# Modulation sums on TensorE in column groups, activations loaded first: a fused transformer block pair, 256 tokens, one core

## The chip, the cores and the metric

The kernel runs on one core of a Trainium2 chip. It is one launch that computes two transformer blocks in float32. The metric is the device time of a launch in microseconds (us); three runs of the kernel before took 879.94 us in the median.

## The reference

Cut to what matters. `c` is one vector of 1024, `x` has 256 tokens of 1024.

```python
c_act = jax.nn.silu(c)
mod = c_act @ w_ada[l] + b_ada[l]                    # w_ada: 1024 x 6144
sh1, sc1, g1, sh2, sc2, g2 = jnp.split(mod, 6, axis=-1)
h = modulate(rms_norm(x, norm1_w[l]), sh1, sc1)      # h * (1 + sc1) + sh1
mix = hybrid_mixer(h, w_in[l], ...)                  # h @ w_in first: q, k, v, z, gates, short conv
x = x + g1[:, None, :] * mix
h = modulate(rms_norm(x, norm2_w[l]), sh2, sc2)
x = x + g2[:, None, :] * swiglu(h, w_ffn_in[l], w_ffn_out[l])
shf, scf = jnp.split(c_act @ w_ada_f + b_ada_f, 2, axis=-1)
...
```

The mixer has a gated delta rule with 8 heads (keys, queries, values, a triangular inverse for each head and half of the tokens), a short convolution branch, and gates. A second block (attention and a gated feed-forward) follows. Nothing of the first block's products with `w_in` can start before `sh1` and `sc1`, which need two of the six column blocks of `w_ada`, 4 MB each.

## The kernel before, in words

All products keep the channels on the 128 partitions and the 256 tokens in the free dimension. A float32 product is made of three matmuls in the faster `fp32r` format: each weight tile is split into a high part `whi` (a copy by ScalarE) and a low part `wlo` (a subtraction by VectorE), and the activations likewise (`h1h`, `h1l` for the first block's input). A tile product is `whi*h1h + whi*h1l + wlo*h1h`. So each unit of work (128 columns of a weight matrix, 8 tiles deep, 24 matmuls) needs one `whi` copy and one `wlo` subtraction of 128x1024 ahead of it. Behind stage one the planner makes these at most five units ahead (`SPL`). Weights come in chunks of up to 1 MB into four buffers `raw` over SyncE's DMA queue, in the order of the list `chunks`; a buffer is loaded again when its last reader is done.

**Stage one** (the loop `for kt in range(KT)`, eight rounds) makes the first input and its first products at once. In round `kt` it takes the 128 columns of `sh1` and of `sc1` that belong to channels `128*kt ...` (chunk `2*kt`, 1 MB of `w_ada`, laid out as [2 vectors, 8 row blocks, 128 columns]) and the 128 rows of `w_in` that those channels multiply (chunk `2*kt+1`). The two sums over 1024 rows are shared by two engines: VectorE multiplies the first 5 or 6 row blocks by `cact` (silu of `c`, one column for each row block) and adds them into `acc` (`gemv_v`, table `gvs`), and TensorE does the remaining row blocks with the weights as the stationary tile and one column of `cact` as the moving one (`gemv`), then adds `acc` over the partitions with a column of ones (`gemv_sum`). `first_mod` adds the bias and makes the scale `a1`. VectorE and ScalarE then make `h1h` and `h1l` for this `kt`, and TensorE adds this channel block's share to six open PSUM banks (`su_mm`, 36 matmuls a round). In the order of the code, round `kt` issues `gemv(kt)`, most of `su_mm(kt-1)`, `gemv_sum(kt)`, the rest of `su_mm(kt-1)`.

**Behind stage one** a planner in Python writes the instruction order: it keeps an estimated clock for each engine (`account`), and between the matmuls of the units it emits what its clock says is ready. Each engine then runs its own list strictly in that order and waits where an operand or a buffer isn't ready. Units follow in the order of the list `units`: the remaining short-convolution columns, the gate columns SCB, two pairs of z, the short-convolution output, the value columns V (with z between), queries Q, gates, and so on. The **later modulation vectors** (`g1`, `sc2`, `sh2`, `g2`, and the two of the last norm) are summed by VectorE alone, four chunks of 1 MB for each vector, two row blocks a chunk: one operation of 128x1024 for each row block into `acc` (`ada_chunk`). `ada_finish` then turns `acc` with eight transposes on TensorE (`sd<-cn,acc`) into two PSUM banks and reduces it with two `TENSOR_REDUCE` into `mod`. Where a chunk stands is set by calls of `sprinkle()` in the list of units. Small PSUM banks for such side work (`sd`) are four and are taken in turn. For the keys, `pair_products` (`sd<-KQ`) and then VectorE's `junk`, `ssk`, `wsc` and `AK` operations run head by head; when all heads are done, `small_inverses` runs 62 small VectorE operations, and later `inverse` (tile `TX`) goes back and forth between TensorE, ScalarE and VectorE.

In the trace nearly every instruction has line L136, the recording helper; so rows are told apart by their tiles.

Of the kernel before, what the change touches and what calls it, by code (L numbers as in the profile page):

```python
# [11 lines left out]
F32 = mybir.dt.float32  # L12
F32R = mybir.dt.float32r
AF = mybir.ActivationFunctionType
OP = mybir.AluOpType
AX = mybir.AxisListType

P = 128
D = 1024
# [51 lines left out]
def body(ctx, tc, a, out):  # L71
# [190 lines left out]
    def bank():  # L262
        i = freeb.popleft()
        return i, pss.tile([P, 512], F32, name=f"sd{i}", tag=f"sd{i}", bufs=1)
# [28 lines left out]
    ones = cst.tile([P, 1], F32, name="ones")  # L293
    V.memset(ones, 1.0)

    colA = cst.tile([P, P], F32, name="colA")
    colB = cst.tile([P, P], F32, name="colB")
    colC = cst.tile([P, P], F32, name="colC")
    colD = cst.tile([P, P], F32, name="colD")
    cact = cst.tile([P, KT], F32, name="cact")  # L300
    mod = cst.tile([P, 8, KT], F32, name="mod")
    a1 = cst.tile([P, KT], F32, name="a1")
# [1260 lines left out]
    def sprinkle():  # L1563
        if later:
            ada_chunk(*later.popleft())
# [12 lines left out]
    for jp in range(4):  # L1578
        pair_units(w_in, SCB0, jp, post_b, h1)
        if jp % 2 == 0:  # L1580
            sprinkle()
    for jp in range(2):
# [3 lines left out]
    for jp in range(4):  # L1586
        pair_units(w_in, V0, jp, post_v, h1)
        if jp < 2:
            pair_units(w_in, Z0, 2 + jp, post_z, h1)
        else:  # L1590
            sprinkle()
    for jp in range(4):
# [51 lines left out]

    load_chunks(1)
    for t in range(2):
        SY.dma_start(xtok[:, t], a["x"][0, t * P:(t + 1) * P, :])
    load_chunks(RAW)
    i, b = bank()
    PE.transpose(b[:, :P], va, ident)  # L1650
# [3 lines left out]
    freeb.append(i)  # L1654
    A.activation(cact, colA[:, 104:112], AF.Silu)

# [3 lines left out]

    def gemv(kt, gv):
        rv = chunks[2 * kt]["v"].rearrange("p (v r) c -> p v r c", v=2)
        i, b = su_b[kt] = bank()
        for v in range(2):
            for r in range(gv, KT):
                PE.matmul(b[:, v:v + 1], rv[:, v, r, :], cact[:, r:r + 1], start=(v == 0 and r == gv), stop=False,
                          skip_group_check=True)

    def gemv_v(kt, r0, r1):
        rv = chunks[2 * kt]["v"].rearrange("p (v r) c -> p v r c", v=2)  # L1670
        ak = ac4[:, kt % 2]
        for r in range(r0, r1):
            if r == 0:
                V.tensor_scalar(ak, rv[:, :, 0, :], cact[:, 0:1], None, op0=OP.mult)
            else:
                V.scalar_tensor_tensor(ak, rv[:, :, r, :], cact[:, r:r + 1], ak, op0=OP.mult, op1=OP.add)

    def gemv_sum(kt):
        i, b = su_b.pop(kt)
        for v in range(2):  # L1680
            PE.matmul(b[:, v:v + 1], ac4[:, kt % 2, v], ones, start=False, stop=True, skip_group_check=True)
        return i, b

    def first_mod(kt, i, b):
        V.tensor_tensor(mod[:, 0:2, kt], b[:, 0:2], colA[:, kt:16:8], OP.add)
        freeb.append(i)
        V.scalar_tensor_tensor(a1[:, kt:kt + 1], mod[:, SC1, kt:kt + 1], 1.0, colA[:, 64 + kt:65 + kt],
                               op0=OP.add, op1=OP.mult)

    gemv(0, 5)  # L1690
    gemv_v(0, 0, 5)
    chunks[0]["free"] = et["V"]
    i, b = gemv_sum(0)
    first_mod(0, i, b)
    ss = wk.tile([P, 2], F32, name="rm", tag="rm")
    rs = wk.tile([P, 2], F32, name="rr", tag="rr")


    scr = slot.tile([P, KT * S + 16], F32, name="scr", tag="L")[:, :D]
    for t in range(2):  # L1700
        A.activation(scr, xtok[:, t], AF.Square, accum_out=ss[:, t:t + 1])
    V.tensor_scalar(ss, ss, 1.0 / D, EPS, op0=OP.mult, op1=OP.add)
# [10 lines left out]
    def x_copied(kp, i, b):  # L1713
        V.tensor_copy(xT[:, 2 * kp:2 * kp + 2].rearrange("p k t -> p (k t)"), b)
        freeb.append(i)

    for kp in range(2):
        x_copied(kp, *x_turned(kp))
    for j in range(3):
        rows(vb, 96 + j * 8, a["sc_conv_w"][0, j], G)  # L1720
# [35 lines left out]
    freeb.append(i)  # L1756
    x_rest = [(kp, *x_turned(kp)) for kp in (2, 3)]
    split_hi(0, (0,))

# [43 lines left out]

    gvs = [5] + [5] * 3 + [6] * 4 + [0]
    for kt in range(KT):
# [3 lines left out]
        if kt:  # L1809
            gemv(kt, gvs[kt])  # L1810
            chunks[2 * kt]["free"] = et["V"]
        load_chunks(2 * kt + 1 + RAW)
        if kt:
            split_hi(kt)
        if kt > 1:
            su_mm(kt - 1, range(NB - 2))
        n1 = n2 = 0
        if kt:
            i, b = gemv_sum(kt)
            low_of(kt, 0)  # L1820
            if 4 <= kt < KT - 1:
                n1, n2 = 0, 1
                gemv_v(kt + 1, 0, n1)
            first_mod(kt, i, b)
# [9 lines left out]
        if kt:  # L1834
            low_of(kt, 1)
        gemv_v(kt + 1, n1, n2)
        V.scalar_tensor_tensor(h1l[:, kt], t, shc, h1h[:, kt].bitcast(F32), op0=OP.add, op1=OP.subtract)
        if not kt:
            low_of(0, 0)
            low_of(0, 1)  # L1840
        if kt < KT - 1:
            gemv_v(kt + 1, n2, gvs[kt + 1])
        give(t)
# [143 lines left out]
```

## Time and profile before

| | before |
|---|---|
| median of 3 runs | 879.94 us (878.63 to 882.96) |
| profiled execution, its own time | 880.14 us |
| its span in the trace | 878.4 us |
| mean granted TensorE clock | 0.988 of full |
| TensorE matmul busy | 841.7 us (96%), 6847 records |
| VectorE busy | 694.2 us (79%) |
| ScalarE busy | 497.9 us (57%) |
| DMA, mean | 202 GB/s |

The time is 1.7 us over the span in the profiled execution. Busy shares are means over stages: TensorE's 96% says that it hardly waits anywhere, and the few places where it does are looked for in windows. A float32 matmul stands in the trace as two records, an `fp32r` matmul or a transpose as one.

### The profile page before, as it was taken

Reading aid. Unit: us, or ns where it says so; the run is one execution under the profiler, and the core shown is the slowest. Engines: PE = TensorE matmul, PEld = TensorE weight load, DVE = VectorE, ACT = ScalarE, POOL = GpSimd, SP = SyncE. Lnnn points to the kernel's source line nnn. Section 1 sums busy time; section 2 is a strip of 40 time slices with the busy share of each in tenths; the row PEclk is TensorE's granted clock in tenths of the full one; section 3 lists DMA queues with packets and bytes.
Section 4 is the critical chain, followed back from the end, with each engine's and each line's share of the span. In section 5 each row is a group of like instructions: output and inputs, shape, how many; then the busy total and the mean of one; then the engine's idle time right before and its main releaser. Section 6 shows DMA issues by size and latency. Waiting matters only on the chain.

```text
span 878.4 us, 17105 instructions
## 1 busy us (share of the span) xinstructions
PE 841.7 (96%) x6847; PEld 812.8 (93%) x6847; DVE 694.2 (79%) x1314; ACT 497.9 (57%) x902; POOL 70.9 (8%) x83
## 2 busy tenths in 40 slices
PE   6999988999999999999999999999999989999995
PEld 6999987999999999999999999998899989999884
DVE  5899998899758889889977555888748988988452
ACT  3349653456656645575554453668656747766341
POOL 3200231000001200200000010200004000000000
PEclk9999998999999999999999999999999989999998
DMA  9995765567724787759988586643425464554611
GB/s 289 317 298 180 247 229 169 168 218 215 240 63 148 230 287 234 261 173 302 326 285 286 169 276 213 207 144 106 136 96 193 132 217 156 192 192 168 199 65 48
DMA packets 158063, 177.35 MB, mean 202 GB/s; under 512 B 9052, under 2 KB 143584, under 8 KB 157984
## 3 DMA queue, kind: packets, MB, share of 16 engines
q1 hardware_dynamic: 156000, 172.57, 61.0%
q0 software_dynamic: 1472, 3.06, 1.1%
q8 instruction: 54, 0.88, 0.4%
q10 hardware_dynamic: 512, 0.62, 0.2%
q14 instruction: 25, 0.20, 0.1%
HBM read 174.64 MB, written 1.60 MB: 201 GB/s over the span
## 4 chain that ended last, share of the span: by engine, by line
PE 56%; issue 22%; DVE 16%; ACT 5%; DMA 1%; POOL 0%; SPq 0%; POOLq 0%; ACTq 0%; DVEq 0%
PE mm L136 48%; PE sd L136 8%; DVE wlo L136 5%; DVE acc L136 3%; DVE cv L136 2%; ACT whi L136 2%; DVE sct L136 1%; DMA raw<-in_w_ada_dram 1%; ACT L136 0%; DVE junk L136 0%; DVE gx L136 0%; DVE AK L136 0%; ACT KQ L136 0%; ACT ct L136 0%; ACT cv L136 0%
## 5 line engine op out<-in xcount | busy, mean ns | idle before, releaser
L136 DVE TENSOR_TENSOR wlo<-raw,whi 128x1024 fp32r<-128x1024 f32 (+2 forms) x267 | 319.3, 1203 | 84.0 <-ACT whi L136 83.6
L136 ACT ACTIVATE whi<-raw 128x1024 fp32r<-128x1024 f32 (+2 forms) x267 | 274.0, 1033 | 152.1 <-PE mm L136 129.0
L136 PE MATMUL mm<-h1h,whi 128*128 128x256 f32 x552 | 159.8, 292 | 0.4 <-ACT h1h L136 0.2
L136 PE MATMUL mm<-h1h,wlo 128*128 128x256 f32 x552 | 153.2, 280 | 1.8 <-DMA raw<-in_w_in_dram 1.3
L136 PE MATMUL mm<-h1l,whi 128*128 128x256 f32 x552 | 153.6, 280 | 0.5 <-DVE h1l L136 0.3
L136 PEld LDWEIGHTS mm<-h1h,whi 128*128 128x128 f32 x552 | 104.6, 191 | 1.7 <-ACT h1h L136 1.1
L136 PEld LDWEIGHTS mm<-h1h,wlo 128*128 128x128 f32 x552 | 103.8, 189 | 2.4 <-DVE wlo L136 2.2
L136 PEld LDWEIGHTS mm<-h1l,whi 128*128 128x128 f32 x552 | 104.0, 189 | 1.4 <-DVE h1l L136 1.1
L136 PE MATMUL mm<-ynh,whi 128*128 128x256 f32 x288 | 82.3, 286 | 4.2 <-DVE gx L136 4.2
L136 PE MATMUL mm<-ynl,whi 128*128 128x256 f32 x288 | 81.8, 284 | 0.0
L136 PE MATMUL mm<-h2nh,wlo 128*128 128x256 f32 x288 | 79.9, 277 | 1.9 <-DVE wlo L136 1.9
L136 PE MATMUL mm<-ynh,wlo 128*128 128x256 f32 x288 | 81.7, 284 | 0.0
L136 PE MATMUL mm<-h2nh,whi 128*128 128x256 f32 x288 | 80.2, 279 | 0.0
L136 PE MATMUL mm<-h2nl,whi 128*128 128x256 f32 x288 | 79.8, 277 | 0.0
L136 DVE SCALAR_TENSOR_TENSOR acc<-raw,cact,acc 128x1024 f32<-128x1024 f32 (+1 forms) x78 | 72.2, 925 | 1.5
L136 PEld LDWEIGHTS mm<-ynh,whi 128*128 128x128 f32 x288 | 55.9, 194 | 4.3 <-issue 4.3
L136 PE MATMUL mm<-xah,whi 128*128 128x258 f32 x192 | 57.2, 298 | 0.0
L136 PEld LDWEIGHTS mm<-h2nh,wlo 128*128 128x128 f32 x288 | 54.1, 188 | 2.1 <-DVE wlo L136 2.1
L136 PEld LDWEIGHTS mm<-ynh,wlo 128*128 128x128 f32 x288 | 55.6, 193 | 0.0
L136 PEld LDWEIGHTS mm<-ynl,whi 128*128 128x128 f32 x288 | 55.4, 192 | 0.0
L136 PE MATMUL mm<-xal,whi 128*128 128x256 f32 x192 | 54.4, 283 | 0.0
L136 PEld LDWEIGHTS mm<-h2nh,whi 128*128 128x128 f32 x288 | 54.3, 189 | 0.0
(335 smaller groups left out, 2107.0 us busy)
## 6 DMA issues: line engine op xcount, KB each, us to landing
raw<-in_w_in_dram SPq DMA_DIRECT2D x30, 1024.0 KB, 5.1
raw<-in_w_ffn_in_dram SPq DMA_DIRECT2D x22, 1024.0 KB, 7.5
raw<-in_w_up_dram SPq DMA_DIRECT2D x22, 1024.0 KB, 5.1
raw<-in_w_ada_dram SPq DMA_DIRECT2D x16, 1024.0 KB, 5.3
raw<-in_w_qkv_dram SPq DMA_DIRECT2D x12, 1024.0 KB, 5.2
raw<-in_w_down_dram SPq DMA_DIRECT2D x10, 1024.0 KB, 5.0
raw<-in_w_ada_dram SPq DMA_DIRECT2D x16, 512.0 KB, 6.5
raw<-in_w_o_dram SPq DMA_DIRECT2D x8, 1024.0 KB, 5.8
```

The costliest lines, as they stand in the source:

```text
L136: r = fn(*args, **kw)
```

## The change: order of loading, TensorE's column groups, and two chunks elsewhere

Three edits. First, the two loads of `x` go ahead of the first `w_ada` chunk on SyncE's queue, and the two squares for the norm are split around the silu, which now writes `cact32`, every value of `cact` 32 times. Second, `gemv` is turned round: 32 equal columns of `cact32` are the stationary tile and the weights move (128 or 256 columns), eight matmuls that write to partitions 0, 32, 64 and 96 in turn (four column groups of the array); ScalarE copies the bank to `acc`, and `gemv_sum` multiplies with `sel`, which has a one at partitions 0, 32, 64 and 96, so that the four groups are added. VectorE's share (`gemv_v`) is gone. In round 0 the eight matmuls are issued for each vector apart, behind the transposes of `x`. Third, the `sprinkle()` of the SCB loop is gone, and that of the V loop runs in all four turns in place of two: the third and fourth chunk of `g1` move there.

```diff
     for jp in range(4):
         pair_units(w_in, SCB0, jp, post_b, h1)
-        if jp % 2 == 0:
-            sprinkle()
...
         if jp < 2:
             pair_units(w_in, Z0, 2 + jp, post_z, h1)
-        else:
-            sprinkle()
+        sprinkle()
...
-    load_chunks(1)
     for t in range(2):
         SY.dma_start(xtok[:, t], a["x"][0, t * P:(t + 1) * P, :])
     load_chunks(RAW)
...
+    A.activation(scr, xtok[:, 0], AF.Square, accum_out=ss[:, 0:1])
...
-    A.activation(cact, colA[:, 104:112], AF.Silu)
+    A.activation(cact32, colA[:, 104:112, None].to_broadcast([P, KT, 32]), AF.Silu)
+    V.tensor_copy(cact, cact32[:, :, 0])
+    A.activation(scr, xtok[:, 1], AF.Square, accum_out=ss[:, 1:2])
...
+    def gemv(kt, vs):
         rv = chunks[2 * kt]["v"].rearrange("p (v r) c -> p v r c", v=2)
-        i, b = su_b[kt] = bank()
-        for v in range(2):
-            for r in range(gv, KT):
-                PE.matmul(b[:, v:v + 1], rv[:, v, r, :], cact[:, r:r + 1], start=(v == 0 and r == gv), stop=False,
-                          skip_group_check=True)
...
+        for r in range(KT):
+            g = 32 * (r % 4)
+            PE.matmul(b[g:g + 32, vs[0] * P:vs[0] * P + w].rearrange("p (v c) -> p v c", c=P), cact32[:, r],
+                      rv[:, vs[0]:vs[0] + len(vs), r], start=(r < 4 and vs[0] == 0), stop=(r >= 4 and vs[-1] == 1),
+                      skip_group_check=True)
+        et["PE"] -= (et["PE"] - t0) * 0.75
+        if vs[-1] == 1:
+            A.activation(ac4[:, kt % 2].rearrange("p v c -> p (v c)"), b[:, 0:2 * P], AF.Copy)
+            chunks[2 * kt]["free"] = et["PE"] + 0.3
...
-            PE.matmul(b[:, v:v + 1], ac4[:, kt % 2, v], ones, start=False, stop=True, skip_group_check=True)
+            PE.matmul(b[:, 256 + v:257 + v], ac4[:, kt % 2, v], sel, start=True, stop=True, skip_group_check=True)
...
         if kt:
-            gemv(kt, gvs[kt])
-            chunks[2 * kt]["free"] = et["V"]
+            gemv(kt, (0, 1))
...
-        gemv_v(kt + 1, n1, n2)
...
-        if kt < KT - 1:
-            gemv_v(kt + 1, n2, gvs[kt + 1])
```

**The start, TensorE's list.** Before (`sd_152` is the bank of the first sums, `rr` the norm's factor, `cn` the identity of a transpose):

```order
L136 MATMUL sd_145<-cn,va 128x128
L136 MATMUL sd_152<-cact,raw 128x1 x6
L136 MATMUL sd_152<-ones,acc 128x1 x2
L136 MATMUL sd_175<-cn,xtok 128x128 x4
L136 MATMUL sd_181<-cn,xtok 128x128 x4
L136 MATMUL sd_209<-cn,rr 128x128 x2
L136 MATMUL sd_213<-cn,xtok 128x128 x4
L136 MATMUL sd_218<-cn,xtok 128x128 x4
L136 MATMUL mm_226<-h1h,whi 128x256 x2
```

The same place of the changed kernel, where `sd_179` is the bank of the first sums:

```order
L136 MATMUL sd_156<-cn,va 128x128
L136 MATMUL sd_167<-cn,xtok 128x128 x4
L136 MATMUL sd_173<-cn,xtok 128x128 x4
L136 MATMUL sd_179<-raw,cact_113 32x128 x8
L136 MATMUL sd_210<-cn,rr 128x128 x2
L136 MATMUL sd_214<-cn,xtok 128x128 x4
L136 MATMUL sd_219<-cn,xtok 128x128 x4
L136 MATMUL sd_179<-raw,cact_113 32x128 x8
L136 MATMUL sd_179<-sel,acc 128x1 x2
L136 MATMUL mm_240<-h1h,whi 128x256 x2
```

The sums of round 0 stood ahead of all transposes of `x`; now their second half and the column sum stand behind all of them, directly ahead of the first products.

**The SCB stretch, VectorE's list.** Before, from one low half on (`sct`, `scl` are the short convolution's, `junk`, `ssk`, `AK` the keys'):

```order
L136 SCALAR_TENSOR_TENSOR junk,ssk<-sd_1468,cn 128x128 x2
L136 TENSOR_SCALAR ssk<-ssk 128x2
L136 TENSOR_TENSOR sct<-mm_1443,sct 128x256
L136 TENSOR_TENSOR scl<-sct,sch 128x256
L136 TENSOR_TENSOR sct<-mm_1495,sct 128x256
L136 SCALAR_TENSOR_TENSOR acc<-raw,cact,acc 128x1024 x2
L136 TENSOR_TENSOR sct<-mm_1524,sct 128x256
L136 TENSOR_TENSOR irk<-ssk,rk 128x2
```

And in the changed kernel:

```order
L136 SCALAR_TENSOR_TENSOR junk,ssk<-sd_1474,cn 128x128 x2
L136 TENSOR_SCALAR ssk<-ssk 128x2
L136 TENSOR_TENSOR sct<-mm_1449,sct 128x256
L136 TENSOR_TENSOR wlo<-raw,whi 128x1024
L136 TENSOR_TENSOR scl<-sct,sch 128x256
L136 TENSOR_TENSOR sct<-mm_1503,sct 128x256
L136 TENSOR_TENSOR wlo<-raw,whi 128x1024
L136 TENSOR_TENSOR sct<-mm_1536,sct 128x256
L136 TENSOR_TENSOR irk<-ssk,rk 128x2
```

Two sums have left this place (two more follow in the list before), and low halves of later units have moved up into it.

**The V stretch, VectorE's list.** Before, where the small inverse has just ended (`cv` are the value columns' convolutions, three operations each):

```order
L136 TENSOR_TENSOR KQ_798<-KQ_798,ct_1914 64x31
L136 TENSOR_TENSOR wlo<-raw,whi 128x1024 x2
L136 SCALAR_TENSOR_TENSOR cv_2589<-mm_2549,colB,cv_2589 128x255
L136 SCALAR_TENSOR_TENSOR cv_2589<-mm_2549,colB,cv_2589 128x254
L136 SCALAR_TENSOR_TENSOR cv_2589<-mm_2549,colB,cv_2589 128x253
L136 TENSOR_TENSOR wlo<-raw,whi 128x1024
```

And in the changed kernel:

```order
L136 TENSOR_TENSOR KQ_802<-KQ_802,ct_1927 64x31
L136 SCALAR_TENSOR_TENSOR cv_2456<-mm_2407,colB,cv_2456 128x255
L136 SCALAR_TENSOR_TENSOR cv_2456<-mm_2407,colB,cv_2456 128x254
L136 SCALAR_TENSOR_TENSOR cv_2456<-mm_2407,colB,cv_2456 128x253
L136 SCALAR_TENSOR_TENSOR acc<-raw,cact,acc 128x1024 x2
L136 TENSOR_TENSOR wlo<-raw,whi 128x1024
L136 SCALAR_TENSOR_TENSOR acc<-raw,cact,acc 128x1024
L136 TENSOR_TENSOR wlo<-raw,whi 128x1024
L136 SCALAR_TENSOR_TENSOR acc<-raw,cact,acc 128x1024
L136 TENSOR_TENSOR wlo<-raw,whi 128x1024 x2
L136 TENSOR_REDUCE mod<-sd_2594 128x4
L136 TENSOR_REDUCE mod<-sd_2600 128x4
```

The four sums and the two reductions now stand right behind the small inverse, ahead of low halves that came first before. From stage one to the 48th low half behind it, the one that VectorE starts at 218.54 us in the trace before, VectorE's list differs by this: 4 `TX` operations of 128x512 more, and 2 convolutions (three operations each) fewer.

## Rows read from the trace of the kernel before

**Rows 1.** The page, part 1: busy us, share of the span, records.

```profile
PE 841.7 (96%) x6847; PEld 812.8 (93%) x6847; DVE 694.2 (79%) x1314; ACT 497.9 (57%) x902; POOL 70.9 (8%) x83
```

**Rows 2.** Windows: stretch, length, busy us of PE PEld DVE ACT POOL, granted clock, DMA.

```profile
24.00:27.00 3.00, 3.00 (x14) 2.79 (x14) 2.86 (x7) 1.58 (x2) 2.65 (x5) 0.50 1.17 310
27.00:60.00 33.00, 32.48 (x277) 31.91 (x276) 29.98 (x70) 10.92 (x17) 0.54 (x1) 1.00 1.02 298
...
126.00:141.00 15.00, 8.81 (x47) 8.10 (x46) 14.41 (x38) 3.93 (x9) 2.98 (x4) 0.77 0.65 212
141.00:165.00 24.00, 24.00 (x212) 23.95 (x211) 17.30 (x45) 13.29 (x19) 1.88 (x3) 1.00 0.54 154
165.00:205.00 40.00, 40.00 (x355) 40.00 (x354) 38.02 (x73) 21.15 (x38) 1.82 (x1) 1.00 0.60 191
```

**Rows 3.** Waits of TensorE from 100 to 230 us: total us, times, longest.

```profile
PE sd L136 <- DVE mod L136: 4.0, 1, 4.0
PE sd L136 <- DVE AK L136: 2.2, 1, 2.2
```

**Rows 4.** Chain that ended last, in stage one: start, us, what.

```profile
15.44 1.87 PE mm L136 x8
...
23.69 4.81 PE mm L136 x24
```

**Rows 5.** Timeline of ScalarE, last rounds of stage one: start, us; idle before, releaser.

```profile
53.76 0.51 ACT L136 ACTIVATE h1h<-gx,mod 128x256 fp32r<-128x256 f32 x1 [3.68 <-DVE gx L136]
...
59.42 0.51 ACT L136 ACTIVATE h1h<-gx,mod 128x256 fp32r<-128x256 f32 x1 [3.68 <-DVE gx L136]
```

**Rows 6.** Groups by form, 16 to 60 us, VectorE's share: count, busy us, mean ns.

```profile
L136 DVE SCALAR_TENSOR_TENSOR acc<-raw,cact,acc 128x256 f32<-128x256 f32 x32 | 15.5, 484 | 1.0
```

**Rows 7.** Timeline of TensorE, 22 us: two rounds' first sums.

```profile
22.04 1.55 PE L136 MATMUL sd<-cact,raw 128*128 128x1 f32 x12
```

**Rows 8.** Timeline of TensorE: float32 matmuls on the whole array, and what follows.

```profile
102.03 1.47 PE L136 MATMUL sd<-KQ 128*128 128x256 f32 x8
103.34 0.39 PE L136 MATMUL sd<-ce,gx 128*128 128x128 f32 x2
```

**Rows 9.** Timeline of TensorE: float32 matmuls in two column groups, and what follows.

```profile
604.40 0.87 PE L136 MATMUL sd<-oatp,oats 128*64 128x256 f32 x8
...
605.20 0.39 PE L136 MATMUL mm<-xah,whi 128*128 128x258 f32 x1
```

**Rows 10.** The tile of those column groups, weight loads: ns min/median/max.

```profile
L136 PEld LDWEIGHTS sd<-oatp,oats x64: 132/136/137, 604.4 to 653.7; 128*64 128x64 f32 x64
```

**Rows 11.** Timeline of the start: TensorE, ScalarE and GpSimd.

```profile
2.23 1.28 ACT L136 ACT_TABLE_LOAD   x1 [2.23 <-DVE ones L136]
...
7.53 1.44 PE L136 MATMUL sd<-cact,raw 128*128 128x1 f32 x6 [0.50 <-DMA raw<-in_w_ada_dram]
...
10.75 1.06 ACT L136 ACTIVATE scr<-xtok 128x1024 f32<-128x1024 f32 x1 [0.17 <-DMA xtok<-in_x_dram]
...
12.18 0.70 POOL L136 TENSOR_TENSOR rr<-rm,nhalf 128x2 f32<-128x2 f32 x1 [11.74 <-DVE rm L136]
...
13.42 1.91 PE L136 MATMUL sd<-cn,xtok 128*128 128x128 f32 x8
...
13.66 0.39 ACT L136 ACTIVATE rows<-sd 128x256 f32<-128x256 f32 x1 [1.76 <-PE sd L136]
```

**Rows 12.** Groups by form on VectorE, 117 to 127.5 us and 135 to 141 us.

```profile
L136 DVE SCALAR_TENSOR_TENSOR acc<-raw,cact,acc 128x1024 f32<-128x1024 f32 x4 | 6.0, 1498 | 0.0
...
L136 DVE TENSOR_REDUCE mod<-sd 128x4 f32<-128x512 f32 x2 | 1.4, 682 | 0.0
```

**Rows 13.** Timeline of VectorE and TensorE, 205 to 220 us: the V stretch.

```profile
205.58 1.51 DVE L136 SCALAR_TENSOR_TENSOR cv<-mm,colB,cv 128x255 f32<-128x255 f32 x3
...
218.54 1.22 DVE L136 TENSOR_TENSOR wlo<-raw,whi 128x1024 fp32r<-128x1024 f32 x1
...
219.81 0.39 PE L136 MATMUL mm<-h1h,wlo 128*128 128x256 f32 x1 [1.25 <-DMA raw<-in_w_in_dram]
```

More of the change, by code (lines that the diff above doesn't have):

```diff
@@ L294, in body @@
     V.memset(ones, 1.0)
+    sel = cst.tile([P, 1], F32, name="sel")
+    V.memset(sel, 0.0)
+    for g in range(4):
+        V.memset(sel[32 * g:32 * g + 1], 1.0)
     colA = cst.tile([P, P], F32, name="colA")
@@ L300, in body @@
     cact = cst.tile([P, KT], F32, name="cact")
+    cact32 = cst.tile([P, KT, 32], F32, name="cact32")
     mod = cst.tile([P, 8, KT], F32, name="mod")
@@ L1648, in body @@
     load_chunks(RAW)
+    ss = wk.tile([P, 2], F32, name="rm", tag="rm")
+    rs = wk.tile([P, 2], F32, name="rr", tag="rr")
+    scr = slot.tile([P, KT * S + 16], F32, name="scr", tag="L")[:, :D]
+    A.activation(scr, xtok[:, 0], AF.Square, accum_out=ss[:, 0:1])
     i, b = bank()
@@ L1659, in body @@
     su_b = {}
-    def gemv(kt, gv):
+    def gemv(kt, vs):
         rv = chunks[2 * kt]["v"].rearrange("p (v r) c -> p v r c", v=2)
-        i, b = su_b[kt] = bank()
-        for v in range(2):
-            for r in range(gv, KT):
-                PE.matmul(b[:, v:v + 1], rv[:, v, r, :], cact[:, r:r + 1], start=(v == 0 and r == gv), stop=False,
-                          skip_group_check=True)
[L1669 to L1676, printed above, removed]
+        if vs[0] == 0:
+            su_b[kt] = bank()
+        b = su_b[kt][1]
+        w = len(vs) * P
+        t0 = et["PE"]
+        for r in range(KT):
[7 more added lines that the diff above has]
+            chunks[2 * kt]["free"] = et["PE"] + 0.3
     def gemv_sum(kt):
@@ L1680, in gemv_sum @@
         for v in range(2):
-            PE.matmul(b[:, v:v + 1], ac4[:, kt % 2, v], ones, start=False, stop=True, skip_group_check=True)
+            PE.matmul(b[:, 256 + v:257 + v], ac4[:, kt % 2, v], sel, start=True, stop=True, skip_group_check=True)
         return i, b
     def first_mod(kt, i, b):
-        V.tensor_tensor(mod[:, 0:2, kt], b[:, 0:2], colA[:, kt:16:8], OP.add)
+        V.tensor_tensor(mod[:, 0:2, kt], b[:, 256:258], colA[:, kt:16:8], OP.add)
         freeb.append(i)
@@ L1688, in first_mod @@
                                op0=OP.add, op1=OP.mult)
[L1690 to L1701, printed above, removed]
     V.tensor_scalar(ss, ss, 1.0 / D, EPS, op0=OP.mult, op1=OP.add)
@@ L1718, in body @@
         x_copied(kp, *x_turned(kp))
+    gemv(0, (0,))
     for j in range(3):
@@ L1757, in body @@
     x_rest = [(kp, *x_turned(kp)) for kp in (2, 3)]
+    gemv(0, (1,))
+    first_mod(0, *gemv_sum(0))
     split_hi(0, (0,))
@@ L1802, in low_of @@
         V.tensor_tensor(wl, rw[:, o * GH:o * GH + n], wh.bitcast(F32), OP.subtract)
-    gvs = [5] + [5] * 3 + [6] * 4 + [0]
     for kt in range(KT):
@@ L1816, in body @@
             su_mm(kt - 1, range(NB - 2))
-        n1 = n2 = 0
         if kt:
@@ L1820, in body @@
             low_of(kt, 0)
-            if 4 <= kt < KT - 1:
-                n1, n2 = 0, 1
-                gemv_v(kt + 1, 0, n1)
             first_mod(kt, i, b)
```

## The prediction, as put on record

> **What bounds the kernel now.** I read the page's busy shares first, then windows, then the waits and the chain inside the windows that stand out. TensorE's matmuls are busy 96% of the span and VectorE 79% [rows 1]. A kernel like this can gain only where TensorE waits, where it runs at the low clock, or where its own work shrinks. The windows show two such places that the change touches. In stage one (16 to 60 us) TensorE is nearly full, 32.48 of 33.00 us between 27 and 60, and VectorE nearly as full, 29.98; from 24 to 27 us the granted clock is 0.50, the lower of the two levels, which costs half of 3 us [rows 2]. DMA is full too (298 GB/s, share 1.02), so three resources are balanced there. The second place is 126 to 141 us, the SCB stretch: TensorE is busy 8.81 of 15 us at a mean clock of 0.77, and VectorE 14.41 of 15. The waits name VectorE: 4.0 us for a `mod` reduction that gives back a small bank, and 2.2 us for an `AK` operation that does the same [rows 3]. Behind it, from 141 to 165 us, VectorE has 6.7 us idle, and from 165 to 205 us it is full again, 38.02 of 40, while TensorE doesn't wait [rows 2]. At 219.81 us TensorE waits 1.25 us; the row names a transfer, but the low half that this matmul reads ended on VectorE at 218.54 + 1.22 = 219.76, so VectorE is the releaser [rows 13].
>
> **Stage one: the work of a round.** Removed from VectorE: 36 sums and 8 first products of 128x256; 32 of the sums take 15.5 us [rows 6]. That frees VectorE, but it ends no wait of TensorE worth more than the 0.5 us of idle between 27 and 60 us. What counts is TensorE's own time. Before, a round's share is 12 records in rounds 0 to 3 and 8 in rounds 4 to 7; 12 take 1.55 us [rows 7], so about 0.125 each. A late round takes 59.42 - 53.76 = 5.66 us [rows 5]; without its 8 records 4.66 us are left for products and the column sum, which stays (two matmuls by `sel` in place of two by `ones`). Rounds 1 to 7 are then 3 x 6.16 + 4 x 5.66 = 41.1 us.
>
> The new sums are eight float32 matmuls of 256 columns, 2048 columns. On the whole array 768 float32 columns take 103.34 - 102.03 = 1.31 us [rows 8], so 2048 in a row would take 3.5 us. Four column groups aren't in the trace before, but two are: the attention's eight records also hold 768 columns (four matmuls, 256 and 128 columns in each half of the array) and the next product starts 605.20 - 604.40 = 0.80 us later [rows 9]. Half of 1.31 is 0.655; so two groups do run side by side, with 0.15 us for going in and out. The bounds for four groups are thus 3.5/4 + 0.15 = 1.02 us and, if only two overlap, 3.5/2 + 0.15 = 1.9 us. Each group has its own output partitions just as the two have, so I take the near end, 1.05 us. Seven rounds become 7 x (4.66 + 1.05) = 40.0 us: **-1.1 us**. The ScalarE copy of the bank (0.39 us for 128x256 [rows 11]) lies beside four banks' worth of products and costs nothing from round 2 on; ScalarE is busy 10.92 of 33 us there [rows 2].
>
> One rule speaks against this. The trace's loads of 64 columns take 0.136 us each [rows 10], and the whole group of eight loads and matmuls takes 0.80 us, less than the matmuls alone would take in a row. The Trainium skill ("TensorE: Matmul & The Clock Gate", Part 3: Packing small matmuls) says that a weight load overlaps with matmuls in flight only when the row group differs; column groups share their rows. By that rule the sums would run in a row with their loads; the trace disagrees for two groups, and no run here shows four.
>
> **Stage one: the start.** `x` now lands where the first `w_ada` chunk landed, by 7.53 us, and that chunk by about 10.75, when the second half of `x` was there before [rows 11]. ScalarE pays a second table load of 1.28 us between its squares. Square, GpSimd's power (1.06 and 0.70 us) and the steps between put the norm's factor near 10.9 us instead of 12.9. But TensorE's list is strict: the second half of round 0's sums stands behind the eight transposes (1.91 us at the low clock) that follow the factor, so it starts near 13.3; at the low clock it takes some 1.0 us, then come the copy (0.39), the column sum and VectorE's and ScalarE's steps to `h1h`, together some 2.8 us more. The first products start near 16.2 to 17.2 instead of 15.44 [rows 4]: **+1.2 us**. If `x` lands earlier the lower end holds. Round 1 is not covered by products of an earlier round: its copy and hand-overs come on top of the 8.25 us between the first and the second products (15.44 to 23.69 [rows 4]), **+0.6 us**. The low clock at 24 to 27 us follows a stretch of one-column matmuls; 256 columns at a time may keep the clock up, worth 1.5 us, and I count half, **-0.7 us**. Stage one then comes to **0.0 us**, from -2.6 (no low clock, early `x`) to +6 (two groups at a time).
>
> **The two chunks: what leaves the SCB stretch.** VectorE loses four sums (6.0 us), two reductions (1.4) and a bias add, 7.5 us [rows 12]; TensorE loses eight transposes, 0.9 us. TensorE's loss there was 6.2 us of idle and (1 - 0.77) x 15 = 3.4 us of clock, of which I count 3 since part fell into the idle. TensorE can come out 10 us earlier, VectorE 7.5 us.
>
> **And what comes back in the V stretch.** The same 7.5 us return behind the small inverse, ahead of low halves that the next units need. So the sum is made at the low half of 218.54 us. Up to it VectorE's list in the change has four `TX` operations more (128x512, nearest row the reduction's 0.68: 2.7 us) and two convolutions fewer (1.51 each: 3.0 us) [rows 12, 13]: 0.3 us less, nothing else. As TensorE waits for that low half, it can be there earlier only by those 0.3 us and by VectorE's idle time that gets used. The idle time is the 6.7 us of 141 to 165, less the 5% that VectorE has between operations even when full (1.98 of 40): 5.5 us. It was idle because weights are split at most five units ahead (`SPL`), so TensorE paces it; TensorE comes 10 us earlier and VectorE 7.5, so 2.5 us of it are used. **-2.8 us**, between -0.3 and -5.8. The other 7.2 us are a new wait of TensorE for low halves, between 180 and 215 us of the new trace. Waits of 2.2 and 4.0 us came with two stretches at the low clock before; the new ones can cost 0 to 3 us in that way, and I take **+1.0**.
>
> SyncE's queue carries the same transfers; the two chunks pass six weight chunks, and the split that reads them isn't late where DMA runs at 154 to 191 GB/s [rows 2]. GpSimd's queue doesn't change.
>
> **Sum.** 0.0 - 2.8 + 1.0 = -1.8 us. Against the profiled execution's own 880.14 us (1.7 over its span) that is 878.3; this execution lies 0.2 over the median of the runs, so I forecast **878.1 us**.
>
> **Rivals.** *The gain stays* (20%): VectorE uses all 5.5 us, no low clock comes in V, and stage one keeps its clock: -5.8 - 2.6, about 871.5. For it speaks that the inverse's `TX` operations have moved up in VectorE's list, so that it has work ready in that idle time; against it that these wait for TensorE and ScalarE in turn, and that splits run only five units ahead. *Column groups overlap only in pairs* (10%): +0.85 us in each of seven rounds, +6, about 884; only the attention's pair is on record. *Loads and groups run in a row* (4%), the mechanism of the page's rule: 3.5 us and 16 loads of half of 0.136, 4.6 us a round, 7 x 3.55 = +25, about 903; rows 9 speak against it. *The V stretch takes more than SCB gave* (11%), on the slower side: the four sums stand in one block ahead of low halves, and the moved-up inverse makes VectorE wait in its list for TensorE and ScalarE; if none of the idle time is used and two low-clock stretches follow, the third term is -0.3 + 3 and round 0 costs its full +1.8: about 884.5. It decides from the point where VectorE is more than 2.5 us later at that low half than I count.
>
> **Numbers.** My forecast's own case has 55%, 874 to 882. Differences under 0.5% (4.4 us) can't be told from no change in this kernel: faster means below 875.5, slower above 884.3. Faster: the 20% and a tenth or so of my own case, 0.32 with the lower part of the uncertain start; slower: 4%, most of the 11% and half of the 10% case, 0.18; the rest, 0.50, is the same. The range from 870 to 885 leaves out the serial groups and the ends of the outer cases.
>
> **What would show it.** In the changed profile: eight-matmul groups of `sd<-cact,raw` near 1.05 us from first start to the next product (1.9 or 3.5 would prove the rivals); first products at 16 to 17 us and the last round's at about 60; no `mod` or `AK` wait at 126 to 141 us; TensorE idle by some 7 us for `wlo` in the V stretch, with VectorE full from stage one to there. I am wrong if TensorE shows no such wait (faster), or if rounds of stage one take 6.5 us (slower).

## The result and the profile after

The changed kernel took 885.83 us in the median of 13 runs (881.56 to 891.09), the kernel before 879.71 (877.67 to 884.68, 13 runs). The ratio is 1.0069, 95% interval 1.0045 to 1.0093: slower by 0.7%, where 878.1 and a range of 870 to 885 were forecast. The profiled execution of the changed kernel took 885.49 us, that of before 880.14; the difference to explain is 5.35 us.

The same stretches as in [rows 2], and the one behind them (same columns), in the changed kernel:

```profile
24.00:27.00 3.00, 1.77 (x24) 0.94 (x20) 1.38 (x3) 1.85 (x3) 1.98 (x4) 1.00 0.66 145
27.00:60.00 33.00, 31.80 (x289) 27.95 (x290) 17.96 (x39) 12.66 (x23) 0.00 (x0) 0.95 0.98 277
126.00:141.00 15.00, 13.42 (x112) 13.07 (x111) 14.51 (x49) 8.18 (x18) 6.92 (x7) 1.00 0.43 140
141.00:165.00 24.00, 24.00 (x214) 24.00 (x213) 17.73 (x47) 12.58 (x20) 0.80 (x1) 1.00 0.71 196
165.00:205.00 40.00, 35.30 (x288) 34.47 (x288) 38.18 (x71) 15.65 (x29) 1.82 (x1) 0.92 0.51 163
205.00:230.00 25.00, 20.45 (x160) 20.28 (x159) 20.10 (x28) 13.48 (x27) 0.00 (x0) 0.85 0.83 267
```

VectorE is down from 30 to 18 us in stage one (27 to 60 us) and TensorE isn't faster for it. The SCB stretch (126 to 141 us) is repaired: 13.4 us of work at full clock where 8.8 us at 0.77 stood. The loss has moved to 165 to 230 us, where TensorE idles and the clock falls. TensorE's waits from 100 to 230 us, which answer to [rows 3]:

```profile
PE sd L136 <- ACT whi L136: 4.6, 1, 4.6
PE mm L136 <- DVE wlo L136: 3.2, 3, 2.5
PE sd L136 <- ACT gx L136: 1.9, 2, 1.1
PE sd L136 <- DVE AK L136: 1.6, 1, 1.6
```

The wait for `mod` is gone, that for `AK` is shorter. To see where time is won and lost, I took the first matmul on the low half of the same unit in both traces. Behind stage one (first unit) it starts at 64.82 us before and 69.16 in the changed kernel: +4.3, and +4.6 a few units later. Behind the SCB stretch (25th unit) it is 152.99 and 148.38: -4.6. Behind the V stretch (68th unit) 315.50 and 322.72: +7.2. So stage one lost 4.6 us, the SCB stretch gained 9.2, the V stretch lost 11.8, and 1.9 us come back by the end (last section). 4.6 - 9.2 + 11.8 - 1.9 = 5.3. These are readings of one profile of each kernel; the runs of the two halves apart (e1 and e2, below) give 2.2 us for the chunks and 4.4 for stage one, in line with them.

**Stage one.** The chain that ended last, 14 to 30 us (as in [rows 4]):

```profile
17.11 1.44 PE mm L136 x8
...
24.23 0.03 ACT acc L136
...
24.51 1.06 ACT whi L136
...
25.59 1.23 DVE wlo L136
26.82 0.08 DVE mod L136
...
28.20 1.96 PE mm L136 x6
```

First products start at 17.11 instead of 15.44, the second at 28.20 instead of 23.69. Ahead of the second stands something that was not there before: ScalarE copies the bank of sums at 24.23, only then makes the split `whi` of round 1, VectorE makes its low half, and only then, in its list, comes `mod`. The split's data had long been loaded; it stood behind the copy in ScalarE's list, and the copy waited for TensorE.

From then on a round is about as long as before: ScalarE's last two `h1h` come at 57.83 and 63.61 us, 5.78 apart, where it was 5.66 [rows 5]. TensorE's timeline, the first sums of an early round (12 records) and of a late one (8), before, and then of a late one after:

```profile
30.20 1.40 PE L136 MATMUL sd<-cact,raw 128*128 128x1 f32 x12
31.45 0.36 PE L136 MATMUL mm<-h1h,whi 128*128 128x256 f32 x1
...
36.23 0.95 PE L136 MATMUL sd<-cact,raw 128*128 128x1 f32 x8
37.03 0.36 PE L136 MATMUL mm<-h1h,whi 128*128 128x256 f32 x1
```

```profile
34.76 1.07 PE L136 MATMUL sd<-raw,cact 128*32 128x256 f32 x16
35.77 0.39 PE L136 MATMUL mm<-h1h,whi 128*128 128x256 f32 x1
```

From the first start to the next product the column groups take 35.77 - 34.76 = 1.01 us; the one-column sums took 0.80 in a late round and 1.25 in an early one.

**The V stretch.** SyncE's timeline (issues of transfers) in the changed kernel, and what SyncE waited for from 185 to 205 us:

```profile
160.71 0.37 SPq L334 DMA_DIRECT2D raw<-in_w_ada_dram  x1
170.73 4.33 SPq L334 DMA_DIRECT2D raw<-in_w_in_dram  x2
178.64 0.37 SPq L334 DMA_DIRECT2D raw<-in_w_ada_dram  x1
185.65 0.37 SPq L334 DMA_DIRECT2D raw<-in_w_in_dram  x1
190.79 0.37 SPq L334 DMA_DIRECT2D raw<-in_w_ada_dram  x1
200.07 0.37 SPq L334 DMA_DIRECT2D raw<-in_w_in_dram  x1
200.49 0.58 SPq L136 DMA_DIRECT2D blk<-KQ  x1
...
204.73 0.37 SPq L334 DMA_DIRECT2D raw<-in_w_in_dram  x1
206.18 6.41 SPq L136 DMA_DIRECT2D U<-blk  x4
```

```profile
SPq L334 <- DVE acc L136: 9.6, 2, 8.8
```

The first two `w_ada` rows are the moved chunks of `g1`, the third is the first of `sc2`. Their sums stand behind the small inverse in VectorE's list, from 197.45 us on. By 190.79 us three of the four weight buffers hold modulation chunks: that of the first from its issue at 160.71 until VectorE is done with it at 200.05. The next weights are issued at 200.07 and 204.73, each within 0.03 us of the end of a pair of sums. ScalarE then waits for transfers twice, 6.4 and 5.0 us, and the transfers of the inverse stand behind these issues on SyncE: `blk<-KQ` at 200.49, though VectorE had made its data by 196.1, and the four `U` behind it from 206.18. VectorE's timeline, where it waits:

```profile
157.45 0.20 DVE L136 TENSOR_TENSOR ct<-KQ,KQ 64x31 f32<-64x31 f32 x1 [3.78 <-DMA KQ<-blk]
...
206.52 2.36 DVE L136 TENSOR_TENSOR wlo<-raw,whi 128x1024 fp32r<-128x1024 f32 x2 [1.82 <-ACT whi L136]
...
214.92 2.36 DVE L136 TENSOR_TENSOR wlo<-raw,whi 128x1024 fp32r<-128x1024 f32 x2 [2.55 <-ACT whi L136]
...
226.76 2.36 DVE L136 TENSOR_TENSOR wlo<-raw,whi 128x1024 fp32r<-128x1024 f32 x2
```

It waits 3.8 us for the transfer that the small inverse starts with, ahead of all this, and 1.8 and 2.6 us for late splits. The last row is the low half at which the prediction made its sum (218.54 us before).

### The profile page after: what moved, and what is told of

The parts are those of the page before. It is cut to its first block, busy times and chain, and to the rows that moved or that the text cites. A ratio compares the mean times of both kernels' runs of the same rounds, so it can differ in the third digit from the quotient of the medians.

```text
span 883.7 us, 17189 instructions
## 1 busy us (share of the span) xinstructions
PE 840.8 (95%) x6911; PEld 807.2 (91%) x6911; DVE 676.8 (77%) x1276; ACT 504.7 (57%) x913; POOL 73.2 (8%) x83
## 4 chain that ended last, share of the span: by engine, by line
PE 53%; issue 22%; DVE 16%; ACT 4%; DMA 3%; POOL 1%; SPq 0%; POOLq 0%; ACTq 0%; DVEq 0%
PE mm L136 44%; PE sd L136 10%; DVE wlo L136 6%; DVE acc L136 2%; ACT whi L136 2%; DVE ct L136 1%; DVE cv L136 1%; DMA raw<-in_w_in_dram 1%; DVE KQ L136 1%; DMA raw<-in_w_ada_f_dram 1%; DMA KQ<-blk 1%; DMA xtok<-in_x_dram 1%; DVE AK L136 1%; DVE sct L136 0%; DVE scl L136 0%
## 5 line engine op out<-in xcount | busy, mean ns | idle before, releaser
L136 DVE SCALAR_TENSOR_TENSOR acc<-raw,cact,acc 128x1024 f32<-128x1024 f32 x42 | 54.4, 1295 | 1.5 <-DMA raw<-in_w_ada_f_dram 1.2
L136 PEld LDWEIGHTS mm<-h2nl,whi 128*128 128x128 f32 x288 | 54.3, 189 | 0.0
```

The source lines that it names most:

```text
L136: r = fn(*args, **kw)
```

## The experiments

Ratios are to the kernel before, timed beside each run on the same chip.

| run | median us | ratio, 95% interval |
|---|---|---|
| e1_chunks_only | 881.32 | 1.0025, 1.0004 to 1.0046 |
| e2_stage_one_only | 883.85 | 1.0050, 1.0031 to 1.0068 |
| e3_one_group | 902.67 | 1.0265, 1.0229 to 1.0300 |
| e4_split_first | 882.05 | 1.0025, 1.0003 to 1.0046 |
| e5_chunks_to_q | 873.80 | 0.9916, 0.9893 to 0.9939 |
| e6_start_whole | 881.48 | 1.0005, 0.9987 to 1.0023 |
| e7_both | 872.97 | 0.9911, 0.9883 to 0.9939 |
| e8_thin_sums | 883.28 | 1.0038, 1.0020 to 1.0056 |
| e9_no_hold | 880.46 | 1.0025, 1.0008 to 1.0042 |
| e10_none_in_v | 872.91 | 0.9915, 0.9890 to 0.9940 |
| e11_chunk_first | 879.65 | 0.9998, 0.9981 to 1.0015 |
| e12_all | 872.94 | 0.9911, 0.9879 to 0.9942 |

### The halves apart: e1 and e2

e1 is the kernel before with the third edit alone, e2 the changed kernel without it:

```diff
         pair_units(w_in, SCB0, jp, post_b, h1)
-        if jp % 2 == 0:
-            sprinkle()
...
             pair_units(w_in, Z0, 2 + jp, post_z, h1)
-        else:
-            sprinkle()
+        sprinkle()
```

> The kernel before with the third edit alone: the two g1 chunks move from the SCB loop to the V loop, stage one stays as it was. Theory A (both halves of the change lose): the SCB stretch gives 9 to 10 us, but behind the small inverse the V stretch takes them back and more, some 7 us of waits and 4 us at the low clock, with a weight chunk that lands late because a buffer is held by a g1 chunk: about 881 to 883, one to three us slower than before. Theory B (only stage one loses, the chunk move gains as the rows of SCB say): 875 to 878. Unaffected by the choice: the wait for mod and AK at 126 to 141 us is gone in both.

> The changed kernel with the two g1 chunks back in the SCB loop: column groups and activations first, alone. Theory A: first products at 17.1 us, second at 28.2 us, the first unit behind stage one 4 to 4.6 us late, and all of it stays to the end, since VectorE sets the SCB stretch and it is late by as much: 883 to 885. Theory B: the delay is taken up in the SCB stretch, where TensorE waits anyway and VectorE has had less to do in stage one: 880 to 881.

Theory A held in both: 0.25% and 0.50%, which add up to 0.75% beside the whole change's 0.69%. So both halves lose. In e1 the 25th unit is 8.2 us earlier than before and the 68th 1.6 us later: the SCB gain is there and the V stretch takes it back. In e2 the delay of stage one (5.5 us at the first unit) is still 5.8 us at the 68th; the SCB stretch takes up none of it, as VectorE, which sets it, is late by as much.

### Stage one: e3, e4, e6 and e11

e3 writes all eight matmuls to one column group:

```diff
-            g = 32 * (r % 4)
+            g = 0
```

> The changed kernel with all eight matmuls of a round written to the same 32 partitions, one column group, so that no two of them can run side by side; the copy and the column sum take those 32 partitions. If the four groups run side by side in the changed kernel, a round's sums go from 1.01 us to about 3.5 us (2048 columns at the 1.31 us for 768 that the whole array took), seven rounds and the start 19 us more: about 905, or more if the low clock comes. If the 1.01 us had another cause (fewer columns of the array make a matmul shorter by itself), the time stays within 3 us of the changed kernel.

TensorE's timeline of e3, the same place as above:

```profile
36.74 3.64 PE L136 MATMUL sd<-raw,cact 128*32 128x256 f32 x16
40.31 0.39 PE L136 MATMUL mm<-h1h,whi 128*128 128x256 f32 x1
```

3.57 us against 1.01: four column groups side by side are 3.5 times as fast as one, and the kernel without that is 1.9% slower than the changed one. The column groups do what they were meant to do.

e4 moves the splits of round 1 ahead of the bank's copy on ScalarE:

```diff
         if kt == 1:
             su_mm(0, range(NB))
+            split_hi(1)
         if kt:
             gemv(kt, (0, 1))
...
-        if kt:
-            split_hi(kt)
         if kt > 1:
+            split_hi(kt)
             su_mm(kt - 1, range(NB - 2))
```

> The changed kernel with one thing moved: in round 1 ScalarE's two split copies stand ahead of the copy of the bank of sums instead of behind it. Theory A (the bank's copy holds the splits until TensorE has made the sums, the low half on VectorE waits for the split, and mod waits behind the low half): the low half runs near 20 us, the column sum is followed by the second products within 2.2 us instead of 3.5, second products at 26.5 to 27 us instead of 28.2, and 1 to 2 us come off the end if nothing later takes them: 884 to 885 where the changed kernel has 886. Rival: the second products wait for the copy and the column sum in any case and still start at about 28 us, no change.

VectorE's timeline of e4 and TensorE's:

```profile
19.32 1.23 DVE L136 TENSOR_TENSOR wlo<-raw,whi 128x1024 fp32r<-128x1024 f32 x1 [0.21 <-ACT whi L136]
25.01 0.16 DVE L136 TENSOR_TENSOR mod<-sd,colA 128x2 f32<-128x2 f32 x1 [4.46 <-PE sd L136]
```

```profile
24.30 0.61 PE L136 MATMUL sd<-sel,acc 128*128 128x1 f32 x4 [0.50 <-ACT acc L136]
...
26.49 0.38 PE L136 MATMUL mm<-h1h,whi 128*128 128x256 f32 x1 [0.58 <-ACT h1h L136]
```

The low half stands at 19.32 instead of 25.59, the second products follow the column sum by 2.2 us instead of 3.5, and the kernel is 0.44% faster than the changed one. The order on ScalarE was the cause of that part. 882.05 is 2 us below the range expected; the second products and the first unit behind stage one are only 1.7 us earlier than in the changed kernel, and the rest lies within the two intervals.

e6 also makes round 0's sums in one piece, ahead of the second eight transposes:

```diff
-    gemv(0, (0,))
+    gemv(0, (0, 1))
...
+    first_mod(0, *gemv_sum(0))
     x_rest = [(kp, *x_turned(kp)) for kp in (2, 3)]
-    gemv(0, (1,))
-    first_mod(0, *gemv_sum(0))
```

> The changed kernel with the round 1 splits ahead of the bank's copy, as in e4_split_first, and round 0's sums in one piece: eight matmuls of 256 columns, the copy and the column sum ahead of the second set of eight transposes, in place of two pieces with the second behind them. The first w_ada chunk has landed at 9.36 us in the changed kernel, for both pieces. Theory A: the first products start at 13.5 to 14.5 us instead of 17.1, stage one ends 2.5 to 3 us earlier than in e4_split_first: 878.5 to 880. Rival (the weights' transfers or ScalarE's first split hold the first products at 16 us or more, or rounds then wait for transfers): within 1 us of e4_split_first, 881 to 883.

The first products came at 15.32 us, not at 13.5 to 14.5: the sums waited for their chunk until 10.22 and then took 1.93 us, where a later round's take 1.07. The first unit behind stage one starts at 64.18, 0.6 us ahead of before, but the time, 881.48, lies in the rival's range and not in theory A's. e11 puts the first `w_ada` chunk ahead of `x` again:

```diff
+    load_chunks(1)
     for t in range(2):
         SY.dma_start(xtok[:, t], a["x"][0, t * P:(t + 1) * P, :])
```

> As e6_start_whole (round 0's sums in one piece, round 1's splits ahead of the bank's copy, the g1 chunks in the V loop as in the changed kernel), but with the loads in the order of the kernel before: the first w_ada chunk, then the activations; the two squares then stand together behind the silu, with one table load. In e6 the sums of round 0 wait for their chunk until 10.22 us and the first products start at 15.32 us; before, the chunk was there by 7.53 us and the activations by 10.75 us, and the products started at 15.44. If the order of the loads is worth nothing by itself (whichever comes second holds the products): products at 14.8 to 15.6 us, time within 1.5 us of e6, 880 to 883. If the activations first are what helps: products at 16 us or later, 883 or more.

Its products start at 16.04, where 16 or later was to speak for the activations first, but its time, 879.65, is that of e6 within the intervals. The order of the two loads is worth nothing that these runs can show. With this stage one (e6, e11) the kernel ties with the one before; the chunk move's loss of 0.25% (e1) lies in it, so such a stage one may be worth 1 to 2 us, which isn't resolved; e7 and e12 below don't show it.

### The chunks: e5, e8, e9, e10

e8 takes VectorE's time out of the moved sums (64 of 1024 columns), e9 takes the hold on the buffers out (the sums read their own tile). Both leave part of `g1` out. All lists keep their order:

```diff
-                V.scalar_tensor_tensor(acc, raw[:, i, :], cact[:, k:k + 1], acc, op0=OP.mult, op1=OP.add)
+                src = acc if v == G1 and j > 1 else raw[:, i, :]
+                V.scalar_tensor_tensor(acc, src, cact[:, k:k + 1], acc, op0=OP.mult, op1=OP.add)
```

> The changed kernel in which the four sums of the two moved chunks take 64 columns in place of 1024, with every list in the same order and all transfers and buffers as they were; so part of the modulation g1 is left out. Theory A (VectorE's 6 us behind the small inverse are what TensorE waits for, itself and through the buffers that these sums give back): the waits of 9.3 us between 195 and 215 us shrink to 3 us or less, and so do the two stretches at the low clock there: 875 to 879 where the changed kernel has 886. Rival (the two transfers themselves, 1 MB each, make the weights behind them late, whatever VectorE does): the wait of 4.6 us at 214.93 us stays, 883 to 886.

> The changed kernel in which the four sums of the two moved chunks are as long as before but read the sum's own tile in place of the loaded chunk; so part of the modulation g1 is left out. All lists and transfers stand in the same order; only the two buffers are no longer held from the chunk's landing until VectorE comes to it. Theory C (formed on e8_thin_sums: two of the four weight buffers are held for 20 to 40 us by chunks whose sums stand behind the small inverse in VectorE's list, the weights behind them are issued at 200.07 and 204.73 us only, and TensorE waits for these): the issues come 10 us or more earlier, ScalarE's waits of 6.5 and 5.0 us for the transfers of w_in go, TensorE's wait of 4.6 us with them, and the time is 878 to 881 where the changed kernel has 886. Theory A as it was (VectorE's 6 us of sums themselves are what is waited for): the waits stay as they are, 884 to 886.

TensorE's waits from 190 to 222 us in e8, then in e9:

```profile
PE sd L136 <- DMA U<-blk: 5.8, 1, 5.8
...
PE mm L136 <- DVE wlo L136: 0.5, 1, 0.5
```

```profile
PE mm L136 <- DVE wlo L136: 2.5, 1, 2.5
```

With VectorE's work gone the wait for low halves shrinks from 2.5 to 0.5 us, but the long one stays, now named as a wait for the `U` transfers. It was for `U` in the changed kernel too, though the row there names the split `whi`. In e8, whose lists are the same, TensorE starts on `U` before ScalarE is done with the first of the two splits, so it doesn't need them (TensorE's timeline, then ScalarE's):

```profile
212.58 1.94 PE L136 MATMUL sd<-cn,U 128*128 128x128 f32 x8 [5.76 <-DMA U<-blk]
```

```profile
211.81 2.01 ACT L136 ACTIVATE whi<-raw 128x1024 fp32r<-128x1024 f32 x2 [4.70 <-DMA raw<-in_w_in_dram]
```

With the hold gone the long wait is gone and the wait for low halves stays. Of the two late issues of weights one came 14 us earlier (186.13 in place of 200.07), the other hardly (204.02 in place of 204.73). The windows from 190 to 220 us, the changed kernel and then e9, show what that does:

```profile
190.00:220.00 30.00, 21.12 (x145) 20.32 (x144) 24.77 (x42) 12.17 (x25) 0.00 (x0) 0.77 0.66 206
```

```profile
190.00:220.00 30.00, 26.12 (x199) 25.09 (x198) 28.09 (x48) 15.54 (x30) 0.00 (x0) 0.89 0.61 180
```

From the 41st unit to the 68th, that is over the V stretch, the changed kernel lost 11.1 us to the kernel before, e8 9.3 and e9 5.4. The times go the same way (0.31% and 0.44% below the changed kernel), though their intervals overlap and don't rank the two. My theory A, that VectorE's 6 us are what is waited for, fell in its main part: 883.28 is the rival's time. But the rival's reason, the two transfers themselves, falls with e9, which makes them all the same. The hold on the buffers (theory C) is the larger of the two and about half of the V stretch's loss: 5.4 of the 11.1 us stay without it.

e5 leaves two chunks in the V loop and gives two to the Q loop; e10 leaves none in V and gives four each to Q and GA:

```diff
         pair_units(w_in, GB0, jp, post_gb, h1)
-        if jp % 2 == 0:
-            sprinkle()
+        sprinkle()
```

> The kernel before with the third edit done otherwise: the SCB loop gives up its two chunks, the V loop keeps two as before, and the Q loop takes two more (four in place of two). The list of chunks is the same, so the third and fourth of g1 now stand where the first two of sc2 stood, and so on. Theory A (what costs in the V stretch is the VectorE work and the buffers of the two more chunks behind the small inverse): the SCB gain of 8 to 9 us stays, as VectorE has 51 of 70 us busy between 230 and 300 us: 870 to 873. Rival (the V stretch waits anyway, as TensorE comes there earlier than VectorE's list allows): most of the gain goes into new waits before 220 us, 876 to 880.

> The kernel before with no chunk in the SCB loop and none in the V loop; the Q and GA loops take four each in place of two (as e5_chunks_to_q, and two further chunks behind the V stretch). By theory C and by the VectorE work alike nothing is held or added in the V stretch: TensorE's waits of 1.5 to 2.3 us between 195 and 225 us go and 1 to 3 us more than in e5_chunks_to_q are gained, 870 to 873. Rival: the further chunks make weights late in the Q and GA loops in their turn: 874 to 877.

Both beat the kernel before by 0.85%, some 7 us. e5 came out 0.8 us above what theory A gave, well below the rival's 876, and e10 within its range, but no lower than e5 beyond the intervals. TensorE's waits from 100 to 230 us in e5, the longest:

```profile
PE sd L136 <- DVE acc L136: 2.0, 1, 2.0
...
```

In e10 this wait is gone, and the 68th unit comes at 304.82 us, 3.9 us ahead of e5's. By the 75th unit the two are level again, since TensorE now waits behind the V stretch:

```profile
312.55 0.94 PE L136 MATMUL sd<-cn,acc 128*128 128x128 f32 x4 [2.01 <-DVE acc L136]
```

The granted clock is 0.83 from 310 to 320 us there, where it is 1.00 in e5. e12 has the same wait, 2.4 us at 313.64. So, as far as the traces show, what e10 gains in the V stretch it loses behind it, as the rival had it, though by a wait for a modulation sum and not for weights, and the time stayed below the rival's 874.

### Both together: e7 and e12

Stage one as in e6, with the chunks as in e5 (e7) and as in e10 (e12):

> Stage one as in e6_start_whole and the chunks as in e5_chunks_to_q. If the two halves add up: the kernel before, plus what e6's stage one is worth against the stage one of before (from -1 to +1 us at the first unit behind it), minus what e5 gains: 870 to 873. If the earlier low VectorE load of stage one is worth something of its own later (VectorE has 17 us less to do there, but its list cannot run ahead), some us less; the rows give no reason for it.

> Stage one as in e6_start_whole with the chunks placed as in e10_none_in_v (none in the SCB and V loops, four each in the Q and GA loops). Stage one of e6 was worth -0.6 us at the first unit in its profile and +1.5 in that of e7_both; so the time is that of e5 and e10, 871 to 874, if VectorE's lighter stage one brings nothing later. If less VectorE work in stage one shortens the SCB stretch further (there is still a wait of 1.5 us for AK at 129 us): 869 to 871.

872.97 and 872.94, the same as e5 and e10. These are the versions that beat both kernels; the chunks' place makes the gain, and the new stage one adds nothing that can be told from zero.

## Why the prediction was wrong

**"Stage one then comes to 0.0 us"** failed, and this is about half of the miss: 4.6 us, beside 4.4 us of the two chunks (11.8 - 9.2 = +2.6 where -1.8 was forecast). By its terms:
- The rounds, -1.1: only about -0.2 (the second products start 4.5 us late, the first unit behind stage one 4.3). The new sums were forecast at 1.05 and measured 1.01; the old ones were priced too high. "12 take 1.55 us [rows 7], so about 0.125 each" counts to the end of the group's last record, where the new sums are counted to the start of the next product. Counted like that, 12 records took 1.25 us and 8 took 0.80: the early rounds gain 0.24 us, the late ones lose 0.2, and together that is nothing.
- The start, +1.2: measured +1.7. The mechanism (second half of round 0's sums behind the transposes) was right, and e6 takes the delay away. Loading `x` first brought no earlier products, since the chunk that came second then held them. What the prediction calls the low clock at the start is read from the pace alone (eight transposes take 1.91 us, eight at 217.28 us take 0.79); the profile's clock column reads 1.00 there.
- Round 1, +0.6: measured 11.09 - 8.25 = +2.8. The step that fails is "its copy and hand-overs come on top": it adds the copy's own time and not what stands behind the copy in ScalarE's list while it waits. That was round 1's split, behind it VectorE's low half, and behind that `mod`. e4 shows it: with the split ahead the second products follow the column sum 1.3 us sooner. In e6, which has that order too and no low clock there, first and second products are 24.05 - 15.32 = 8.73 us apart, +0.5. That the copy costs nothing from round 2 on held.
- The clock, -0.7: the stretch at the low clock from 24 to 27 us did go, but two others came, and the second follows the new wait ahead of the second products. Windows of the changed kernel:

```profile
17.50:21.50 4.00, 4.00 (x23) 4.00 (x23) 1.81 (x3) 1.04 (x3) 3.42 (x7) 0.57 1.21 299
28.00:31.60 3.60, 3.40 (x14) 3.17 (x15) 1.89 (x3) 1.88 (x4) 0.00 (x0) 0.53 1.12 314
```

**The SCB stretch** was right: 10 us forecast, 9.2 measured (in e1 too), and the wait for `mod` gone; a wait of 1.6 us for `AK` stayed, where none was forecast.

**The V stretch** was right in the size of its idle time and wrong in the cause, so the size is luck. TensorE's waits there sum to 9.25 us against 1.95 before (1.25 and 0.70): 7.3 more, and 7.2 were forecast, all for low halves. Only 2.8 us were for low halves (the 3.2 of the list above include 0.4 at 112 us), 4.6 for `U` and 1.9 for ScalarE's `gx`. Two steps failed:
- "the split that reads them isn't late": I compared the bandwidth [rows 2] with what is loaded, and not how long a buffer is held. A chunk ahead of its sums occupies one of four buffers until VectorE comes to it, and VectorE's list put the small inverse first. e9 shows it.
- "2.5 us of it are used": of VectorE's idle time from 141 to 165 us, 6.7 us before, 24.00 - 17.73 = 6.3 us were still idle, 3.8 of them a wait for the small inverse's transfer, and the waits for late splits came on top. The low half that was forecast 2.8 us earlier came at 226.76 us, 8.2 later; 4.3 us of that had been lost by the first unit behind stage one.

The low clock was mis-sized: 11.8 - 7.3 = 4.5 us where +1.0 was taken; the granted clock was 0.77 over 190 to 220 us, where it was 1.00 before. It was low around and behind each of the two long waits, the one that ended at 201.23 us (for a low half) and the one that ended at 214.93 (for `U`):

```profile
198.00:205.60 7.60, 5.04 (x24) 4.84 (x25) 6.67 (x6) 1.16 (x3) 0.00 (x0) 0.56 0.59 189
212.00:219.00 7.00, 4.07 (x19) 4.10 (x20) 4.38 (x7) 4.06 (x8) 0.00 (x0) 0.54 0.62 175
```

As an estimate from these rows, 5.04 us of work at 0.56 and 4.07 at 0.54 lose 2.2 and 1.9 us, so the two stretches weigh about the same.

The slower rival (the V stretch takes more than SCB gave) came true on its own account, 11.8 against 9.2: hardly any of the idle time was used and two stretches at the low clock followed, as it said, but about half of the loss came by the held buffers, which it didn't name; and stage one's loss came on top. That rival was given 11%, and the loss in stage one was in the range only as "two groups at a time", which e3 rules out.

What stays open: what the 5.4 us are made of that the V stretch still loses in e9. Its wait of 2.5 us for the low half behind the sums is one part. In e5, where two chunks fewer stand in the V loop, the same stretch loses 0.6 us, so the chunks are the cause of the whole; no run with the changed kernel's lists takes the hold and the sums away together.

## What to carry to other kernels

Ask of a moved load not only whether the bandwidth is free, but from when to when it occupies a buffer: from its issue to the end of its last reader, and the reader's place in its engine's list decides that. Ask of an added small operation (here a copy of 0.4 us) not what runs beside it, but what stands behind it in the same list while it waits. And where work is taken off a stretch, put it where its engine has idle time and no long block ahead: the two chunks taken out of the SCB loop cost 0.25% when they went to the V loop and gained 0.85% when two went to the Q loop.

## What the runs showed of the hardware

The same stage one ran in e6 and e7. From 16 to 32 us, e6 and then e7:

```profile
16.00:32.00 16.00, 14.78 (x141) 12.45 (x141) 7.71 (x14) 6.93 (x12) 7.20 (x14) 1.00 1.11 311
```

```profile
16.00:32.00 16.00, 14.78 (x116) 12.99 (x118) 7.41 (x14) 5.68 (x10) 7.21 (x14) 0.89 1.06 301
```

Equal busy time, 141 matmuls against 116: one execution had a stretch at the low clock there, the other had none, and the first unit behind stage one came at 64.18 and at 66.28 us. A difference of 2 us at that place between two profiles says nothing by itself, and neither does e6's 0.6 us.

TensorE's products go at one of two paces without any wait, at the same granted clock. From 760 to 800 us before, and from 765 to 805 us, the same units within some us, in the changed kernel:

```profile
760.00:800.00 40.00, 40.00 (x343) 40.00 (x342) 34.62 (x58) 27.60 (x45) 0.00 (x0) 1.00 0.58 185
```

```profile
765.00:805.00 40.00, 40.00 (x355) 40.00 (x355) 35.35 (x60) 28.82 (x45) 0.00 (x0) 1.00 0.58 186
```

Both are fully busy, but 355 records against 343: a product every 0.113 us or every 0.118. Such stretches last some 10 to 80 us and fall differently in the profiles; here they give the changed kernel some 3 us back late, and take 1.4 between 345 and 430 us. What starts them no run shows.
